# An encoder layer on one core: the first gate's weight parts without a hold, and split by GpSimd

## The chip, the cores and the metric

The kernel runs on one core of one Trainium2 chip. The core has a matrix engine (TensorE, PE in the profile), a vector engine (VectorE, DVE), an activation engine (ScalarE, ACT), a general engine (GpSimd, POOL) and a queue engine that only issues transfers (SyncE, SP). Each engine takes its own instructions strictly in order; semaphores make one wait for another. The metric is the device time of one execution in microseconds (us), lower is better.

## The reference

One bidirectional encoder layer is applied to two sequences of 1024 positions and 1024 channels, in float32. With `p = rmsnorm(x) @ w_in` cut into a Fourier value, a Fourier gate, three Hyena inputs, a Hyena gate and two merge gates, it computes

```
fz  = real(fft over positions and, per group of 256, over channels)(fv)
y_f = (fz * silu(fg)) @ w_fourier_out
v, x1, x2 = short_conv(hv)                 # width 3
z   = x2 * long_conv(x1 * long_conv(v, k0), k1)   # filters k from a small network
y_h = (z * silu(hg)) @ w_hyena_out
out = (sigmoid(mg_f) * y_f + sigmoid(mg_h) * y_h) @ w_out
y   = x + rmsnorm(out, g_post)
```

Every one of the large products has 1024 x 1024 weights per section of `w_in`, and is needed nearly exact, so each operand is kept as two parts: a rounded one (`h`) and the remainder (`l`), and a product is three matmuls, h*h, h*l and l*h.

## The kernel before

The work is traced in program order, and a planner puts it in an order per engine before the run: it keeps its own reckoning of when each operand is there, and on each engine takes the earliest-traced instruction that is ready by that reckoning. The chip then runs each engine's list in order. Four stages follow one another in the program, but the lists overlap them:

- `phase_fourier` (line 489): for both sequences, the normalized and transposed input, the Fourier values and their transforms, written to DRAM (`d_x`, `d_fz`). Its last part, called the tail here, is the second half of the second sequence: `stage` (line 423) and the channel transform (lines 458 to 487), a chain of small matmuls on TensorE, copies on ScalarE (lines 434, 475, 476) and sums on VectorE.
- The filter stage, the first loop of `phase_main` (line 928): the first sequence's input is loaded back in 8 pieces and split into `xh`, `xl` by `load_x` (line 711: cast on ScalarE, subtraction on VectorE); then 16 filters are made (`filter_taps`, `filter_spectrum`), and between them 30 gate tiles (`spill_gate`, line 793) fill TensorE. `fill` (line 925) spreads the gate tiles over the 16 rounds; round 0 has one of them, the first tile of section 5, and `self.opening` is true in that round alone.
- `branches` (line 977): the long convolutions of both sequences, with the projections between them.
- `phase_blocks` (line 1044): the second sequence's remaining projections and the output products, in an order written out by hand.

A gate tile is one call of `inproj` (line 739): two PSUM tiles (`pin`, tag `mm` with four buffers), and for each half of the weights (`q`, 512 columns) a raw tile `wr` of 256 KB fetched by SyncE into one of two buffers, a pair of rooms for its parts, and 24 matmuls that read the parts and `xh`, `xl`. The rooms rotate over four pairs (`rooms`, line 724): `wh`/`wl` twice, then two pairs called `whl` elsewhere. The parts of the first sequence's tiles are made in lines 762 to 764: ScalarE rounds the raw weights to `h`, ScalarE writes `-h` into `l`, and a transfer issued by GpSimd's queue adds the raw weights onto `l` from DRAM.

In the opening round the two ScalarE instructions stand in a block `issue_after(self.rows.ins)` (line 761), which orders them on ScalarE behind one given instruction. `self.rows` is set in line 476, each time the tail's second scaled copy `Pm` is traced; when the gate tile is traced it is the last one of the whole Fourier stage.

`split` (line 168) is the other way to make parts: a cast on ScalarE, then a subtraction raw - h on a named engine.

Of the kernel before, what the change touches and what calls it, by code (L numbers as in the profile page):

```python
# [12 lines left out]
AF = mybir.ActivationFunctionType  # L13
# [148 lines left out]
class K:  # L162
# [223 lines left out]
    def fourier_half(self, b, half, W, fo, px, pf, begun={}):  # L386

        nc = self.nc
        WE, WO = W

        def pair(shape, tag, bufs=1):
            return [pf.tile(shape, F32R, tag=f"{tag}{i}", name=f"{tag}{i}", bufs=bufs) for i in range(2)]
# [30 lines left out]
        def stage(np_, data, e, edge, out, tag):  # L423

            pe = self.psum(tag, 2, "pse")[0:np_, :258]
            po = self.psum(tag, 2, "pso")[0:np_, :258]
            for m in range(4):
                last = (edge is None and m == 1) or m == 3
                self.mm3(pe if m < 2 else po, data(m), (seq[:, 0, e, m], seq[:, 1, e, m]), m % 2 == 0, last)
                if m == 1 and edge is not None:  # L430
                    self.mm(pe.rearrange("p (a b) -> p a b", a=3), edge, al, False, True)
            ev = pf.tile([P, 258], F32, tag="sev", name="sev", bufs=1)[0:np_]
            st = pf.tile([P, 514], F32, tag="sst", name="sst", bufs=1)[0:np_]
            nc.scalar.copy(ev, pe)
            self.add("dve", st[:, 0:258], ev, po)
            if e == 0:
                self.sub("dve", st[:, 512:257:-1], ev[:, 0:255], po[:, 0:255])
            else:
                self.stt("dve", st[:, 512:257:-1], ev[:, 0:255], -1.0, po[:, 0:255])
            nc.vector.tensor_copy(st[:, 513:514], st[:, 0:1])  # L440
            if len(out) == 2:
                self.split(out[0], out[1], st, "dve", "act")
            else:
                nc.scalar.copy(out[0][0:34], st)
                self.sub("dve", out[0][32:34], st[32:34], out[0][32:34])
        ch, cx = fo["chan"], fo["chx"]
        vec = self.vec
# [6 lines left out]
        for g in range(2):  # L454
            Pp, Qp = PP[g], pair([P, 514], "qp")
            co = slice(P * g, P * g + P)
            stage(P, lambda m: (OO[0][:, m, co], OO[1][:, m, co]), 1, None, Qp, "XT"[g])
            A = pf.tile([P, 1026], F32, tag="fA", name="fA", bufs=1)
            B = pf.tile([P, 1026], F32, tag="fB", name="fB", bufs=1)
            gg = 2 * half + g  # L460
            for n in range(2):
                w = (258, 256)[n]
                ns = slice(258 * n, 258 * n + w)
                pr, qr = (Pp[0][:, ns], Pp[1][:, ns]), (Qp[0][:, ns], Qp[1][:, ns])
                pP = self.psum("X", 2, "pP")[:, :w]
                self.mm3(pP, (ch[:, 0, 0:P], ch[:, 1, 0:P]), pr, True, False)
                self.mm(pP, cx[:, 0, g, :], PX[:, ns], False, True)
                pQ = self.psum("X", 2, "pQ")[:, :w]
                self.mm3(pQ, (ch[:, 0, P:2 * P], ch[:, 1, P:2 * P]), qr, True, False)
                self.mm(pQ, ch[:, 0, 2 * P:3 * P], pr[0], False, False)  # L470
                self.mm(pQ, ch[:, 0, 2 * P:3 * P], pr[1], False, False)
                self.mm(pQ, cx[:, 1, g, :], PX[:, ns], False, True)
                Ps = pf.tile([P, 258], F32, tag="fPs", name="fPs", bufs=2)
                Pm = pf.tile([P, 258], F32, tag="fPm", name="fPm", bufs=1)
                nc.scalar.copy(Ps[:, :w], pP)
                self.rows = nc.scalar.activation(Pm[:, :w], pP, AF.Copy, scale=vec[:, 11:12])
                t0 = 258 * n
                w = (258, 255)[n]
                r = slice(0, w)
                self.stt("dve", A[:, t0:t0 + w], pQ[:, r], vec[:, 10:11], Ps[:, r])  # L480
                self.add("dve", B[:, t0:t0 + w], pQ[:, r], Pm[:, r])
                w = (258, 254)[n]
                r = slice(0, w)
                self.stt("dve", A[:, 1024 - t0:1024 - t0 - w:-1], pQ[:, r], vec[:, 11:12], Ps[:, r])
                self.stt("dve", B[:, 1024 - t0:1024 - t0 - w:-1], pQ[:, r], vec[:, 12:13], Pm[:, r])
            nc.gpsimd.dma_start(self.d_fz[b][2 * gg], A[:, 0:1024])
            nc.gpsimd.dma_start(self.d_fz[b][2 * gg + 1], B[:, 0:1024])
# [251 lines left out]
    def inproj(self, sec, mt, b=None, plain=False):  # L739

        nc, a = self.nc, self.a
        ps = [self.psum("mm", 4, f"pin{n}") for n in range(2)]
        for q in range(2):
            s = slice(512 * q, 512 * q + 512)
            src = a["w_in"][sec, mt][:, s]
            kept = self.d_w[sec - 1][mt] if b is not None else None
            if b or plain:
                h, l = [self.wp.tile([P, 512], F32R, tag=g, name=g, bufs=2) for g in ("wh", "wl")]
            else:
                h, l = self.rooms()  # L750
            if b:
                self.keep_parts()
                for t, k in zip((h, l), kept):
                    nc.sync.dma_start(t.bitcast(F32), k[:, s])
            else:
                r = self.wp.tile([P, 512], F32, tag="w", name="wr", bufs=2)
                nc.sync.dma_start(r, src)
                if plain:
                    self.split(h, l, r, "dve", "act")
                else:  # L760
                    with self.tc.issue_after(self.rows.ins) if self.opening else ExitStack():
                        nc.scalar.copy(h, r)  # L762
                        nc.scalar.mul(l, h, -1.0)
                    nc.gpsimd.dma_start(l, src, accum_op=ADD)
                    self.keep_parts()
                    if kept:
                        self.unsaved = [(t, k[:, s]) for t, k in zip((h, l), kept)]
            h, l = [t.rearrange("p (a b) -> p a b", a=4) for t in (h, l)]
            for n in range(2):
                for kk in range(4):  # L770
                    k = 4 * q + kk
                    s = slice(512 * n, 512 * n + 512)
                    self.mm3(ps[n], (h[:, kk], l[:, kk]), (self.xh[k][:, s], self.xl[k][:, s]), k == 0, k == 7)
        return ps
# [741 lines left out]
```

## Time and profile before

| | |
|---|---|
| median of three runs | 2438.34 us (2437.77 to 2440.07) |
| the profiled execution | 2444.92 us, its span 2443.1 us |
| TensorE busy | 2371.6 us, 97% of the span |
| VectorE busy | 1986.3 us, 81% |
| ScalarE busy | 1177.0 us, 48% |
| GpSimd busy | 449.3 us, 18% |
| bytes moved | 499.65 MB, mean 205 GB/s |

The span is the time from the first to the last instruction of the profiled execution; the time of that execution holds a little around it. Busy shares are means over stages, so the stretches in the prediction are read beside them. A row of the timeline has the start in us from the span's start, the duration in us, engine, line, operation, output and inputs, the shape, and in brackets the idle time of the engine before it with what ended it; rows that follow one another are merged with a count. Rows of groups have the count, total busy time and mean ns of one. Lines of helpers (171 and 181 for the split's cast and subtraction, 177, 194 for every matmul) stand for all that call them, so the tile's name tells which work it is.

### The profile page before, as it was taken

To read this page: it belongs to the slowest core of one execution; us is meant where nothing else is said; L and a number is where in the kernel's file an instruction comes from. 1 tells how busy PE (TensorE), PEld (TensorE's weight loads), DVE (VectorE), ACT (ScalarE), POOL (GpSimd) and SP (SyncE) were. 2 spreads that over 40 slices of the span, in tenths; PEclk is the share of its full clock that TensorE was granted. 3 is DMA by queue.
4 is the path that set the end of the run, shared out by engine and by line. 5 is a ranking of instruction groups with operands and counts; after the bars stand their busy time and mean duration, and the time that the engine had idled before them with its cause. 6 is when DMAs were issued, how large, how long until landed. Compare 5 with 4: busy or idle time off the path is not lost. (4 is left out here: it accounts for less than half of the span.)

```text
span 2443.1 us, 37244 instructions
## 1 busy us (share of the span) xinstructions
PE 2371.6 (97%) x13006; PEld 2058.6 (84%) x13006; DVE 1986.3 (81%) x3840; ACT 1177.0 (48%) x2220; POOL 449.3 (18%) x568
## 2 busy tenths in 40 slices
PE   5998899999999999999999999999999999999998
PEld 4987788888888888888888888888888888888786
DVE  7687777777776899899899999998667687778777
ACT  5545677776754444343332322333334375656543
POOL 1331111111122232321124444310000000101000
PEclk9998899999999999999999999999999999999999
DMA  8544876777777767665455666553646687978744
GB/s 319 171 160 173 239 198 193 202 203 198 214 213 236 203 201 203 190 180 167 172 181 181 217 208 214 190 172 135 215 147 216 213 306 248 279 263 228 224 155 155
DMA packets 262980, 499.65 MB, mean 205 GB/s; under 512 B 26550, under 2 KB 90263, under 8 KB 262408
## 3 DMA queue, kind: packets, MB, share of 16 engines
q1 hardware_dynamic: 220076, 380.53, 46.7%
q0 software_dynamic: 42528, 116.72, 18.3%
q8 instruction: 102, 1.67, 0.3%
q14 instruction: 86, 0.70, 0.1%
q10 hardware_dynamic: 188, 0.02, 0.0%
HBM read 333.59 MB, written 167.77 MB: 205 GB/s over the span
## 5 line engine op out<-in xcount | busy, mean ns | idle before, releaser
L194 PE MATMUL pin<-xh,wl 128*128 128x512 f32 x1024 | 401.7, 394 | 3.0 <-DMA wl<-in_w_in 2.4
L194 PE MATMUL pin<-xh,wh 128*128 128x512 f32 x1024 | 403.2, 394 | 0.9 <-ACT wh L762 0.9
L194 PE MATMUL pin<-xl,wh 128*128 128x512 f32 x1024 | 402.8, 393 | 0.0
L194 PE MATMUL pin<-xh,whl 128*128 128x512 f32 x896 | 292.4, 396 | 0.0
L194 PEld LDWEIGHTS pin<-xh,wl 128*128 128x128 f32 x1024 | 193.8, 189 | 38.8 <-DMA wl<-in_w_in 2.6
L194 PEld LDWEIGHTS pin<-xh,wh 128*128 128x128 f32 x1024 | 194.0, 190 | 36.1 <-ACT wh L762 1.2
L194 PEld LDWEIGHTS pin<-xl,wh 128*128 128x128 f32 x1024 | 193.9, 189 | 35.0
L194 PEld LDWEIGHTS pin<-xh,whl 128*128 128x128 f32 x896 | 167.7, 189 | 32.5
L194 PE MATMUL pT<-cinv,yh 128*128 128x256 f32 x1024 | 192.8, 283 | 2.3 <-ACT yh L171 2.3
L194 PE MATMUL pin<-xl,whl 128*128 128x512 f32 x448 | 177.7, 397 | 0.0
L194 PEld LDWEIGHTS pT<-cinv,yh 128*128 128x128 f32 x1024 | 165.5, 191 | 12.4 <-ACT yh L171 2.7
L194 PE MATMUL pX<-bh,cfwd 128*128 128x256 f32 x768 | 159.5, 288 | 1.1 <-ACT bh L171 1.1
L181 DVE TENSOR_TENSOR t<-pX,k 128x1024 f32<-128x1024 f32 x128 | 156.1, 1219 | 4.0 <-PE pX L194 3.1
L171 ACT CAST yh<-y 128x512 fp32r<-128x512 f32 x128 | 79.3, 620 | 158.1 <-DVE y L181 120.4
L194 PE MATMUL pT<-cinv,yl 128*128 128x256 f32 x512 | 145.6, 284 | 0.0
L171 ACT CAST bh<-b 128x512 fp32r<-128x512 f32 x144 | 88.9, 619 | 105.9 <-DVE b L181 69.6
L194 PEld LDWEIGHTS pX<-bh,cfwd 128*128 128x128 f32 x768 | 126.1, 192 | 4.8 <-ACT bh L171 1.6
L181 POOL TENSOR_TENSOR draw<-draw 128x256 f32<-128x256 f32 x96 | 92.4, 963 | 114.8 <-DMA draw<-in_w_out 39.8
L181 DVE TENSOR_TENSOR bl<-b,bh 128x512 fp32r<-128x512 f32 x144 | 101.3, 706 | 12.0 <-ACT bh L171 11.9
L194 PE MATMUL pX<-bl,cfwd 128*128 128x256 f32 x384 | 109.7, 286 | 0.0
L181 DVE TENSOR_TENSOR yl<-y,yh 128x512 fp32r<-128x512 f32 x128 | 90.6, 708 | 16.4 <-ACT yh L171 16.2
L194 PEld LDWEIGHTS pT<-cinv,yl 128*128 128x128 f32 x512 | 98.2, 192 | 1.9
(366 smaller groups left out, 6091.9 us busy)
## 6 DMA issues: line engine op xcount, KB each, us to landing
k<-d_k SPq DMA_DIRECT2D x128, 512.0 KB, 4.4
wr<-in_w_in SPq DMA_DIRECT2D x136, 256.0 KB, 3.5
d_g<-gt SPq DMA_DIRECT2D x92, 256.0 KB, 3.5
d_k<-kt SPq DMA_DIRECT2D x128, 128.0 KB, 2.8
d_k<-kt SPq DMA_DIRECT2D x64, 256.0 KB, 2.5
fz<-d_g SPq DMA_DIRECT2D x64, 256.0 KB, 5.5
wl<-in_w_in POOLq DMA_DIRECT2D x56, 256.0 KB, 5.2
whl<-in_w_in POOLq DMA_DIRECT2D x56, 256.0 KB, 5.4
```

What stands on the lines that cost most here:

```text
L171: self.rounded = nc.scalar.copy(h, src)
L181: return e.tensor_tensor(out, a, b, op=op)
L194: return self.nc.tensor.matmul(out, lhsT, rhs, start=start, stop=stop, skip_group_check=shared)
```

## The change

In the opening round the first gate tile's parts are now made by `split` with a subtraction on GpSimd. The hold behind the Fourier stage's last scaled copy is gone, and so are, for the two halves of this one tile, the negation on ScalarE and the accumulating transfer. All other gate tiles are made as before. The later tiles of the second sequence (`plain`) keep VectorE for the subtraction.

```diff
@@ fourier_half
-                self.rows = nc.scalar.activation(Pm[:, :w], pP, AF.Copy, scale=vec[:, 11:12])
+                nc.scalar.activation(Pm[:, :w], pP, AF.Copy, scale=vec[:, 11:12])
@@ inproj
                 r = self.wp.tile([P, 512], F32, tag="w", name="wr", bufs=2)
                 nc.sync.dma_start(r, src)
-                if plain:
-                    self.split(h, l, r, "dve", "act")
+                if plain or self.opening:
+                    self.split(h, l, r, "dve" if plain else "pool", "act")
                 else:
-                    with self.tc.issue_after(self.rows.ins) if self.opening else ExitStack():
-                        nc.scalar.copy(h, r)
-                        nc.scalar.mul(l, h, -1.0)
+                    nc.scalar.copy(h, r)
+                    nc.scalar.mul(l, h, -1.0)
                     nc.gpsimd.dma_start(l, src, accum_op=ADD)
                     self.keep_parts()
```

## The prediction

> **What bounds the kernel now.** First the page: engine totals, and the strip of 40 slices of 61 us each.
>
> ```profile
> span 2443.1 us, 37244 instructions
> ...
> PE 2371.6 (97%) x13006; PEld 2058.6 (84%) x13006; DVE 1986.3 (81%) x3840; ACT 1177.0 (48%) x2220; POOL 449.3 (18%) x568
> ...
> PE   5998899999999999999999999999999999999998
> ...
> PEclk9998899999999999999999999999999999999999
> ```
>
> TensorE is busy for 97% of the span, so work taken off it counts one for one wherever it never waits. Its clock dips in two slices only, the fourth and fifth (183 to 305 us), which is where the edited weights are used. So the next view is busy time by stretches around that place; the columns are the stretch, its length, PE, PEld, DVE, ACT and POOL busy with counts, the granted clock, the DMA share and GB/s.
>
> ```profile
> 200.00:210.00 10.00, 10.00 (x86) 10.00 (x85) 5.08 (x15) 3.24 (x8) 1.10 (x2) 1.00 0.14 55
> 210.00:220.00 10.00, 5.95 (x46) 5.21 (x45) 5.64 (x12) 5.65 (x11) 1.05 (x2) 1.00 0.85 278
> 220.00:230.00 10.00, 7.80 (x48) 6.94 (x48) 8.89 (x19) 7.32 (x12) 0.00 (x0) 0.83 1.01 388
> 230.00:240.00 10.00, 5.41 (x20) 4.32 (x20) 9.54 (x19) 6.71 (x14) 0.71 (x2) 0.54 0.55 195
> 240.00:250.00 10.00, 6.61 (x31) 5.94 (x32) 8.15 (x21) 5.88 (x15) 1.06 (x2) 0.67 0.36 125
> 250.00:260.00 10.00, 8.54 (x29) 6.56 (x28) 5.14 (x14) 8.23 (x20) 4.81 (x7) 0.59 0.68 205
> 260.00:270.00 10.00, 7.78 (x22) 6.15 (x23) 8.51 (x20) 2.36 (x7) 0.40 (x1) 0.66 1.07 318
> 270.00:280.00 10.00, 10.00 (x57) 8.69 (x56) 6.39 (x18) 7.55 (x19) 1.75 (x2) 1.00 0.84 292
> ...
> 720.00:760.00 40.00, 40.00 (x209) 34.12 (x208) 18.06 (x46) 21.02 (x39) 10.08 (x16) 1.00 0.89 268
> ...
> 1400.00:1500.00 100.00, 100.00 (x616) 89.64 (x615) 99.03 (x168) 29.76 (x56) 46.96 (x60) 1.00 0.65 216
> ```
>
> The Fourier tail is a hole in TensorE's work, and from 270 us it is full again. Between 220 and 270 us the idle time is 2.20 + 4.59 + 3.39 + 1.46 + 2.22 = 13.9 us. On top the busy time ran slow: busy times (1 - clock) gives 1.3 + 2.5 + 2.2 + 3.5 + 2.6 = 12.1 us. So about 26 us of full-rate TensorE time are lost in these 50 us. What ends the waits, in the view of waits of PE for 205 to 270 us:
>
> ```profile
> PE pQ L194 <- DVE fB L177: 5.1, 3, 2.1
> PE pft L194 <- ACT sev L434: 2.4, 1, 2.4
> PE pin L194 <- DMA wl<-in_w_in: 2.4, 1, 2.4
> ```
>
> The tail hops TensorE, ScalarE, VectorE and back with nothing to fill in between. The gate's matmuls (`pin`) would be filler, and the hold keeps them out: on ScalarE the last held-to row is L476, and the casts follow it at once.
>
> ```profile
> 250.94 0.45 ACT L476 ACTIVATE fPm<-pP,vec 128x256 f32<-128x256 f32 x1
> 251.30 1.13 ACT L762 CAST wh<-wr 128x512 fp32r<-128x512 f32 x2
> ...
> 253.13 1.14 ACT L763 ACTIVATE wl<-wh 128x512 fp32r<-128x512 f32 x2
> ```
> ```profile
> 193.74 1.21 SPq L757 DMA_DIRECT2D wr<-in_w_in  x2
> ...
> 251.93 5.67 SPq L757 DMA_DIRECT2D wr<-in_w_in  x4
> ```
> ```profile
> wr<-in_w_in SPq DMA_DIRECT2D x136, 256.0 KB, 3.5
> ```
>
> The raw weights were fetched at 193.74 us and lay for 57 us; with two raw buffers only, the next gate's weights are not fetched before 251.93 us.
>
> **The change, part by part.**
>
> *Casts no longer held.* Two casts leave 251.30 us for some point after the raw weights land, about 198 us (issued by 194.95, 3.5 us to landing at the median). ScalarE has room: 6.76 us idle in 200 to 210 alone against 1.13 us. On the path: 0; without that cover, 1.1 us. The matmuls can't follow at once, though. They read the transformed input, whose second parts VectorE makes in eight pieces, first and last:
>
> ```profile
> 221.91 1.23 DVE L181 TENSOR_TENSOR xl<-xl,xh 128x1024 fp32r<-128x1024 f32 x1
> ...
> 234.91 1.22 DVE L181 TENSOR_TENSOR xl<-xl,xh 128x1024 fp32r<-128x1024 f32 x1
> ```
>
> So the first gate can run from 223.1 us, piece by piece until 236.1 us. Its PSUM tag `mm` is free by then: the last holder of the tail is read at 209.93 us.
>
> ```profile
> 209.93 0.42 DVE L181 TENSOR_TENSOR oo<-pfv,oo 128x256 fp32r<-128x256 f32 x1 [1.44 <-ACT oo L171]
> ```
>
> What a gate costs TensorE comes from its own matmuls when they finally run:
>
> ```profile
> 262.22 0.80 PE L194 MATMUL pin<-xh,wl 128*128 128x512 f32 x1 [2.37 <-DMA wl<-in_w_in]
> ...
> 268.36 0.39 PE L194 MATMUL pin<-xh,wh 128*128 128x512 f32 x1
> ...
> 269.98 0.39 PE L194 MATMUL pin<-xl,wh 128*128 128x512 f32 x1
> ```
>
> Fourteen start between 262.22 and 268.36 us, 0.44 us each at the low clock; seven steps lead from 268.36 to 269.98 us, 0.231 us each at full. A gate is 2 halves x 2 row halves x 4 blocks x 3 products = 48 matmuls: 48 x 0.231 = 11.1 us, or 21 us cold. The room from 220 to 250 us is 10.2 us idle plus 6.0 us of slow clock, 16.2 us; so it fits if the filler also brings the clock back. Term: -11.1 us. Bounds: 0, if the matmuls end up where the tail could have run anyway; the whole 11.1 for this gate.
>
> The clock first as the rows show it: in the ten us from 220 its mean is 0.83, behind two gaps of 2.13 and 2.05 us, and it came back after 6.1 us of unbroken matmuls.
>
> ```profile
> 214.28 0.63 PE L194 MATMUL pQ<-qp,chan 128*128 128x256 f32 x3 [2.13 <-DVE fB L177]
> ...
> 220.13 0.51 PE L194 MATMUL pse<-alt,x5t 128*128 128x258 f32 x2 [2.05 <-DVE x5t L181]
> ```
>
>  The Trainium skill (TensorE: Matmul & The Clock Gate, "What's actually happening") says that the clock halves after an idle window of about 3.4 us and is restored after as long a busy one. By that rule only some 8 of the gate's matmuls would run slow rather than 14, and the sum would be better by 6 x 0.21 = 1.3 us; the rows show the slower return.
>
> *The following gate.* Two raw buffers that come free near 203 us instead of 252 us let the next gate's fetches, casts, negations and accumulating transfers start some 45 us earlier (they keep the old form). Such a transfer lands in 3.8 to 9.1 us in this stretch of the kernel:
>
> ```profile
> L764 POOL DMA_DIRECT2D wl<-in_w_in x17: 867/872/1261, 254.1 to 477.9; - x17
> ...
> DMA to landing us min/median/max: 3.8/5.1/9.1
> ```
>
> So this gate's 48 matmuls may fill what the first leaves: 16.2 - 11.1 = 5.1 us up to 250 us, and 3.7 idle + 6.1 slow = 9.8 us from 250 to 270 us. Bounds 0 and 14.9 us. I take 5, a third: the order is made by a planner in advance, and the transfer shares the DMA engines with the input's eight loads (share 0.85 and 1.01 between 210 and 230 us).
>
> *Second parts by GpSimd.* Removed: two negations on ScalarE (1.14 us for both), two issues on POOL (0.87 each) and two accumulating transfers, with TensorE's wait of 2.4 us for the first; that wait lies in the 26 us and isn't counted again. Added: two GpSimd subtractions of 128x512. None with this output is in the trace; the nearest rows, and GpSimd's first row after the fetch:
>
> ```profile
> L181 POOL TENSOR_TENSOR x<-x,sg 128x512 f32<-128x512 f32 x16 | 38.2, 2400 | 38.5 <-ACT sg L1007 38.4
> ...
> L181 POOL TENSOR_TENSOR eo<-xg 128x512 f32<-128x512 f32 x8 | 15.4, 1938 | 7.8 <-ACT xg L347 5.1 <-DVE sst L440 1.3 <-DVE el L181 1.3
> ...
> L181 POOL TENSOR_TENSOR wo<-wor,wo 128x256 fp32r<-128x256 f32 x16 | 14.4, 913 | 21.1 <-ACT wo L171 21.1
> ```
>
> ```profile
> 207.46 0.57 POOL L486 DMA_DIRECT2D d_fz<-fA  x1 [19.97 <-DVE fA L177]
> ```
>
> 1.83 us (twice the 256-wide row, the same form) to 2.40 us each; I take 1.9, so 3.8 us together. POOL has nothing for 20 us before 207.46 us, so nothing queues behind them; if they came after, the `d_fz` transfers issued at 207.46 us would wait up to 4 us, and with them the buffers fA and fB. What they can disturb is VectorE: the 260-wide sum there takes 0.42 us alone and up to 0.97 beside GpSimd.
>
> ```profile
> L181 DVE TENSOR_TENSOR wer<-wfv x6: 418/564/966, 172.8 to 188.6; 128x260 f32<-128x260 f32 x6
> ```
>
> At worst VectorE loses half of 4.8 us, 2.4 us; between 200 and 210 us alone it idles 4.9 us. Term 0, bounds 0 and +2.4. On VectorE such a subtraction takes 0.71 us, 1.2 less than on GpSimd:
>
> ```profile
> L181 DVE TENSOR_TENSOR bl<-b,bh 128x512 fp32r<-128x512 f32 x144 | 101.3, 706 | 12.0 <-ACT bh L171 11.9
> ```
>
> The Trainium skill (GPSIMD Engine Reference, "4.1 Engine selection") advises VectorE for such work, GpSimd taking about twice as long for two inputs. The trace agrees (2.7 times); by that rule 2.4 us are lost if both halves lie on the path, which with some 20 us to spare before 223 us they don't.
>
> *Whether the gain lasts.* One more stretch, from the middle of the filter stage:
>
> ```profile
> 400.00:500.00 100.00, 100.00 (x537) 86.27 (x537) 77.87 (x196) 70.51 (x154) 12.22 (x14) 1.00 0.76 209
> ```
>
> From 270 us on TensorE is full, in the filter stage as later, so work done early is time saved, unless another engine then sets the pace. VectorE works only 18.06 of 40 us between 720 and 760 us: there it waits for TensorE, with 21.9 us to give. Hence a head start up to about 22 us reaches the next stage whole.
>
> Sum: -11.1 - 5 + 0 = -16 us. Against its own execution, 2444.92 us with a span of 2443.1, that is 2429; the three timed runs lie 6.6 us lower (2438.34), so I predict 2422. A measurement here can't tell less than 0.2%, 4.9 us, from no change: faster means below 2433.5, slower above 2443.2.
>
> **Rivals.**
>
> *All of the hole is filled* (0.08): both gates warm and the third begins; the gain goes to 22 to 26 us, held by VectorE's 21.9. 2438.3 - 25 = 2413. For it: free rooms and PSUM. Against: DMA share.
>
> *Only part of the first gate* (0.18): the pieces of input come every 1.9 us, each worth 6 matmuls; TensorE stays under 60% and cold, the gate takes 21 us of a 10 us idle room. About half of 11.1 plus the saved 2.4 us wait: -8, 2430.
>
> *Given back* (0.14): the head start is lost where VectorE is the bound. For it: 99.03 of 100 us busy at 1400 to 1500 us. Against: the slack at 720 us moves VectorE's work forward too. 2438.
>
> *Slower* (0.18): TensorE takes its queue in order, and the planner places the gate's matmuls by loads as it reckons them. If it reckons the input pieces or the second gate's transfers earlier than they land, matmuls that wait for them stand ahead of the tail's. The tail's 29 us after 223 us then start as late as 236 (+13), and two transfers at 9.1 rather than 3.8 us add 10.6; less the 11.1 us of matmuls, +12.5 at most, taken as +8: 2446. It decides from waits above 11 us. For it: VectorE is 89 to 95% busy making those pieces. Against: the plan before had only one such wait, 2.4 us.
>
> **How the numbers follow.** The forecast has 0.42, with 2414 to 2430 as its own range. Faster is 0.42 + 0.08 + 0.18 = 0.68, same 0.14, slower 0.18. The range runs from 2411 (just past the filled hole) to 2443, leaving 0.05 below and 0.13 above.
>
> **What would show it.** Right: casts `wh` near 200 us on ScalarE, two GpSimd rows `wl<-wr,wh` of about 1.9 us before 207 us, `pin` matmuls from 223 us, clock back at 1.00 before 240 us, the third fetch of `wr` before 212 us, and the same order of work afterwards some 16 us sooner. Wrong: a clock still at 0.6 between 230 and 260 us (part only), long waits of PE for `xl` or `whl` (slower), or a full hole with the gaps opening behind 760 us (given back).

## The result, and the profile after

The changed kernel takes 2436.53 us (median of 22 runs, 2433.34 to 2440.61); the kernel before, run beside it, takes 2441.05 us (22 runs, 2434.41 to 2446.73). The ratio is 0.9982, with a 95% interval of 0.9975 to 0.9989: 4.4 us faster, just under the 4.9 us that the prediction took as the least difference to be told. It forecast 16 us. The profiled execution took 2440.61 us, the longest of the 22, with a span of 2438.8; that of the kernel before, 2444.92 us, lies as far above its median, so this one pair of profiles shows about the same, 4.3 us.

The page of the kernel after: span, engine totals, TensorE's strip and the strip of its clock.

```profile
span 2438.8 us, 37250 instructions
...
PE 2365.9 (97%) x13006; PEld 2055.1 (84%) x13006; DVE 1992.5 (82%) x3840; ACT 1173.9 (48%) x2216; POOL 444.1 (18%) x568
...
PE   5998999999979999999999999999999999999998
...
PEclk9999999999989999999999999999999999999999
```

The clock's dip in the fourth and fifth slices (183 to 305 us) is gone, though TensorE's own digit in the fourth is still 8. A new dip stands in the twelfth, 671 to 732 us, in TensorE's digit and in the clock. The stretches of the kernel after, in the columns used in the prediction (stretch, length, PE, PEld, DVE, ACT, POOL busy with counts, granted clock, DMA share, GB/s):

```profile
210.00:220.00 10.00, 5.01 (x42) 4.80 (x41) 3.42 (x9) 1.50 (x4) 1.20 (x3) 0.87 0.89 263
220.00:230.00 10.00, 9.46 (x58) 8.47 (x59) 6.92 (x16) 7.81 (x15) 1.05 (x2) 0.79 0.73 277
230.00:240.00 10.00, 10.00 (x56) 8.59 (x55) 9.65 (x17) 8.79 (x13) 0.72 (x2) 1.00 0.80 300
240.00:250.00 10.00, 10.00 (x54) 8.61 (x54) 5.07 (x11) 4.61 (x10) 1.79 (x2) 1.00 0.76 229
250.00:260.00 10.00, 10.00 (x53) 8.53 (x52) 4.50 (x12) 8.36 (x18) 1.98 (x3) 1.00 0.84 233
260.00:270.00 10.00, 10.00 (x56) 8.72 (x55) 4.78 (x12) 6.31 (x14) 1.52 (x2) 1.00 0.62 186
...
640.00:680.00 40.00, 34.55 (x189) 29.66 (x188) 33.71 (x94) 26.42 (x65) 6.11 (x8) 0.94 0.62 170
680.00:720.00 40.00, 30.95 (x152) 26.77 (x152) 33.21 (x79) 21.45 (x46) 2.88 (x4) 0.77 0.38 115
720.00:760.00 40.00, 40.00 (x215) 34.31 (x215) 26.97 (x72) 22.28 (x45) 10.68 (x16) 1.00 0.97 287
```

And one stretch of the kernel before, which the prediction did not look at:

```profile
640.00:720.00 80.00, 80.00 (x421) 68.61 (x420) 64.49 (x160) 49.05 (x105) 16.84 (x23) 1.00 0.75 207
```

The prediction's own measure, idle time plus busy time times (1 - clock), is called lost time from here on. From 210 to 270 us it falls from 30.1 us to 8.2: in each of the four stretches from 230 us on the change leaves TensorE full at full clock. That is 21.9 us won. Between 640 and 720 us, where the kernel before loses nothing, the kernel after idles 5.45 + 9.05 = 14.5 us and runs 34.55 x 0.06 + 30.95 x 0.23 = 9.2 us' worth of slow clock: 23.7 us lost. Between them the two places leave the kernel after 1.8 us behind; that it is faster all the same comes from stretches that neither the edit nor the prediction was about (the table).

Lost time by stage, summed in this way over stretches of 10 to 100 us of each kernel's profile, is the table on which the experiments rest. The span less all lost time is 2350 to 2356 us in every one of the fourteen kernels, so the lost time accounts for the span to about 6 us. Its size depends a little on the stretches, since the clock is a mean over each: cut into stretches of 10 us, the 23.7 us become 21.3.

| lost us in | 0–210 | 210–270 | 270–600 | 600–800 | 800–1600 | 1600–end | span |
|---|---|---|---|---|---|---|---|
| before | 33.7 | 30.1 | 0 | 0 | 10.1 | 16.2 | 2443.1 |
| after | 36.1 | 8.2 | 0 | 23.7 | 4.2 | 15.7 | 2438.8 |

The rows add up to 90.1 and 87.9 us, so the table holds 2.2 of the 4.3 us; the largest term in favour of the kernel after, behind the hole, is 800 to 1600 us, which no experiment explains.

What happens at 640 to 720 us. Most of TensorE's idle time there, by the view of its waits for that stretch of the kernel after (what waits, for what; us, times, the longest):

```profile
PE pft L194 <- DVE T L181: 9.8, 4, 5.8
PE pXf L194 <- ACT w3s L171: 2.4, 1, 2.4
PE pXf L194 <- DVE bl L181: 1.5, 1, 1.5
```

`pft` and `pXf` are the filter network's small matmuls; they wait for VectorE's and ScalarE's steps of the same chain. There is no filler left between them: from 668.01 to 697.81 us every matmul of TensorE is the filter network's. The end of the filler shows in the timelines of the kernel after: the last gate tile ahead of the two projections is copied out at 638.18 us, the last matmul of the two projections is issued at 667.78 us, and the projections' four PSUM tiles are read only from 689.82 us, behind a sum of the filter's own work.

```profile
638.18 0.59 ACT L801 COPY gt<-pin 128x512 f32<-128x512 f32 x1 [2.13 <-PE pin L194]
...
689.82 1.27 ACT L783 ACTIVATE v<-pin,wsh 128x512 f32<-128x512 f32 x2 [1.79 <-DVE fO L181]
```
```profile
667.78 0.39 PE L194 MATMUL pin<-xh,whl 128*128 128x512 f32 x1
```

The kernel before copied that same gate tile 38 us later:

```profile
676.33 0.59 ACT L802 COPY gt<-pin 128x512 f32<-128x512 f32 x1 [2.13 <-PE pin L194]
```

The filters went the other way. Each filter's taps end in a sum `fE` on VectorE, behind which its spectrum is made; the first and the last of the 16, before and then after:

```profile
259.20 1.21 DVE L181 TENSOR_TENSOR fE<-T,T 128x1024 f32<-128x1024 f32 x1
...
702.91 1.22 DVE L181 TENSOR_TENSOR fE<-T,T 128x1024 f32<-128x1024 f32 x1
```
```profile
280.50 1.22 DVE L181 TENSOR_TENSOR fE<-T,T 128x1024 f32<-128x1024 f32 x1
...
716.67 1.23 DVE L181 TENSOR_TENSOR fE<-T,T 128x1024 f32<-128x1024 f32 x1
```

So the gates finish 38 us sooner and the filters 14 us later. The time from the last gate's copy ahead of the projections to the last filter's sum, called the gap from here on, grows from 702.9 - 676.3 = 26.6 us to 716.7 - 638.2 = 78.5 us. The theory to be tested (the gap theory): for the length of the gap TensorE has only two projections and the filters' small matmuls to do; past some length it starves and its clock falls. Rivals: the PSUM tiles that the two projections hold block gates that could run; the GpSimd subtraction rather than the missing hold delays the filter chain; or VectorE's load in later stages takes the gain back, as the prediction's own rival had it.

### The profile page after: what moved, and what is told of

It reads as the page before. It is cut to its first block, busy times and chain, and to the rows that moved or that the text cites. A ratio compares the mean times of both kernels' runs of the same rounds, so it can differ in the third digit from the quotient of the medians.

```text
span 2438.8 us, 37250 instructions
## 1 busy us (share of the span) xinstructions
PE 2365.9 (97%) x13006; PEld 2055.1 (84%) x13006; DVE 1992.5 (82%) x3840; ACT 1173.9 (48%) x2216; POOL 444.1 (18%) x568
## 5 line engine op out<-in xcount | busy, mean ns | idle before, releaser
L181 POOL TENSOR_TENSOR draw<-draw 128x256 f32<-128x256 f32 x96 | 98.1, 1022 | 112.8 <-DMA draw<-in_w_out 38.7
L181 DVE TENSOR_TENSOR bl<-b,bh 128x512 fp32r<-128x512 f32 x144 | 104.2, 726 | 14.6 <-ACT bh L171 14.5
```

The lines of the kernel that those rows point to most:

```text
L181: return e.tensor_tensor(out, a, b, op=op)
```

## The experiments

All kernels compute the complete result; only order and the making of parts differ. Ratios are to the kernel before, run on the same chip.

**Which of the two edits.** `unhold_only` drops the hold and leaves the parts to negation and accumulating transfer; `hold_pool` keeps the hold on the cast and makes the second part on GpSimd.

```diff
unhold_only, against before:
-                    with self.tc.issue_after(self.rows.ins) if self.opening else ExitStack():
-                        nc.scalar.copy(h, r)
-                        nc.scalar.mul(l, h, -1.0)
+                    nc.scalar.copy(h, r)
+                    nc.scalar.mul(l, h, -1.0)
hold_pool, against after (line 476 sets self.rows again, as before):
-                    self.split(h, l, r, "dve" if plain else "pool", "act")
+                    with ExitStack() if plain else self.tc.issue_after(self.rows.ins):
+                        nc.scalar.copy(h, r)
+                    self.sub("dve" if plain else "pool", l, r, h)
```

> The hold is taken away, the parts are still made by negation and accumulating transfer; the result is complete. If the hold alone matters, the hole between 228 and 270 us is filled as in the changed kernel (TensorE busy 10 of 10 us from 230 us, clock 1.00) and the ratio to the kernel before is within 0.2% of the changed kernel's 0.998. If GpSimd's subtraction is what lets the gate start early, the first gate's matmuls wait for transfers that land 4 to 9 us after their issue and the ratio is 1.000 or above.

> The hold on the rounding cast stays, the second parts are made by GpSimd's subtraction. Only the wait of 2.4 us for the first accumulating transfer near 262 us can go; the hole stays. Ratio to the kernel before 0.999 to 1.000 if the hold is what matters; 0.998 if the subtraction is.

Measured: `unhold_only` 2436.57 us against 2443.3, ratio 0.9971 (0.9961 to 0.9982); `hold_pool` 2442.96 us, 1.0004 (0.9995 to 1.0014). In the profile of `unhold_only` 8.5 us are lost from 210 to 270 us and 23.4 us from 600 to 800, with a gap of 714.7 - 636.8 = 78 us: the whole picture of the change. `hold_pool` has 24.7 and 0, with a gap of 26.6 us; the 5.4 us that its hole loses less than before are lost again behind it (5 to 6 us from 270 to 600 us). So the hold alone does it, the gain and the giving back, and GpSimd's subtraction brings nothing that can be told. The rival that blamed the subtraction falls.

**PSUM or the gap.** `after_gates_first` traces the last round's two gate tiles one round sooner, ahead of the two projections, so that they need no tile that the projections hold. `before_gates_first` does it to the kernel before.

```diff
+            cut = lambda i: i * len(fill) // nf if i < nf - 1 else len(fill)
...
-                for sec, c in fill[i * len(fill) // nf:(i + 1) * len(fill) // nf]:
+                for sec, c in fill[cut(i):cut(i + 1)]:
```

> The changed kernel, with the last round's two gate tiles traced in the round before, ahead of the first two convolution projections. Theory 1 (the gain is lost because those two projections sit in all four PSUM tiles until filter 14 gives back its tap tiles, and TensorE has no filler from 668 to 712 us): the 14.5 us of idle time and about 9 us of slow clock between 640 and 720 us go, 22 us of gate matmuls fill them, ratio 0.990 to 0.994. Theory 2 (the filters start 21 us later and the last of them, at 717 us, sets when the next stage begins, whatever fills the time before): ratio 0.997 to 0.999, the last filter again at about 717 us.

> The kernel before, with the same two gate tiles moved ahead of the projections. There TensorE is full from 270 to 800 us, so there is no idle time to win back: both theories expect 0.998 to 1.002. A gain like that of the changed kernel with this edit would say that the edit is worth its gain by itself and not as the return of a lost head start.

Measured: `after_gates_first` 2437.3 us, 0.9982 (0.9973 to 0.9991), and `before_gates_first` 2442.28 us, 0.9999 (0.999 to 1.0007). Neither is told apart from the kernel that it was made of. In `after_gates_first` the last gate is copied at 668.2 us instead of 638.2, but the loss only falls from 23.7 to 16.2 us, for the last filter ends still later; neither expectation had that. Stretches and last sum of `after_gates_first`:

```profile
640.00:680.00 40.00, 37.33 (x201) 32.01 (x199) 28.04 (x77) 28.75 (x57) 8.41 (x12) 1.00 0.81 233
680.00:720.00 40.00, 33.79 (x151) 27.48 (x151) 32.60 (x79) 26.84 (x62) 8.66 (x13) 0.83 0.60 170
```
```profile
731.97 1.22 DVE L181 TENSOR_TENSOR fE<-T,T 128x1024 f32<-128x1024 f32 x1
```

Here no gate is left for a held tile to block, and still 16.2 us are lost: the tiles can't be the main cause. They do have a part. In the kernel after the next gate's first matmul is issued at 697.81 us, when the last reading of a held tile by VectorE ends (697.01 + 0.74 us); but at most the 7.5 us that the edit saves can be put down to them. The two gates' work, some 22 us by the prediction's 11.1 each, bought 7.5 us in the stage, since it pushed the last filter 15.3 us later, from 716.67 to 731.97 us.

**Gates traced a round later.** If the filters lose because the gates stand in their way, giving the filters the earlier place in the trace should help. `after_gates_later1` and `after_gates_later2` shift all gates by one and two rounds, `before_gates_later1` does it to the kernel before.

```diff
+            cut = lambda i: max(i - 1, 0) * len(fill) // nf if i < nf else len(fill)
...
-                self.opening = i == 0
-                for sec, c in fill[i * len(fill) // nf:(i + 1) * len(fill) // nf]:
+                for sec, c in fill[cut(i):cut(i + 1)]:
+                    self.opening = (sec, c) == fill[0]
```

> The changed kernel, with every gate tile traced one filter round later, so that the planner prefers the next filter to a gate. Theory 2 (the gates took the lead of the filters; the filters, which start 21 us later and keep 29.5 us a round, end the stage, with TensorE short of work from 640 to 720 us): the filters run ahead again, the last one is at 700 us or earlier, no idle time between 640 and 720 us, ratio to the kernel before 0.990 to 0.995. Theory 1 (only the PSUM tiles held by the first two projections keep the late gates out): those projections are still ahead of four gates, so TensorE still idles there, ratio 0.997 to 1.000.

> The same by two rounds: a second dose. Theory 2: filters still earlier, ratio 0.988 to 0.995; if the gates then run out of time behind the last filter, six of them stand at the end with nothing of the filters to cover and the ratio rises to that of one round or above. Theory 1: 0.997 to 1.002.

> The kernel before with the gates one round later: the control. It keeps the hole at 210 to 270 us, and its TensorE is full in the filter stage, so theory 2 expects 0.998 to 1.002. A gain here as large as with the change would mean that the order of gates and filters is worth it by itself.

Measured: 1.0063 (1.0047 to 1.0079), 1.0132 (1.0115 to 1.0148) and 1.0049 (1.0036 to 1.0062): slower, all three. This missed. The first filter's sum of `after_gates_later1` is at 279.0 us, hardly sooner than 280.5, so the place in the trace is not what put the gate ahead of it. And the shift leaves only 26 gates ahead of the projections where there were 28, so the last of them is copied at 607.1 us and the gap grows to 101 us, with 37.9 us lost from 600 to 800 (55.9 in `after_gates_later2`). `before_gates_later1` holds the useful point: its last filter ends at 703.6 us, as in the kernel before, only the last gate comes sooner (648.0), the gap is 56 us, and 7.9 us are lost where the kernel before loses none.

**The gap from the other side.** `before_filter_late` leaves the gates of the kernel before alone and delays the filters, by holding the copy of the filter network's hidden layer behind the Fourier tail.

```diff
-            nc.scalar.copy(self.hid, hid)
+            with tc.issue_after(self.rows.ins):
+                nc.scalar.copy(self.hid, hid)
```

> The kernel before with one thing delayed: ScalarE's rounding of the hidden layer, which every filter matmul reads, is held behind the tail as the gate is (251 us in place of 215). The first filter's matmuls then start at about 253 us in place of 233 and its sums come at 275 to 282 us in place of 259, without any filler brought forward. If the late first filter is what the stage pays for at its end, TensorE runs short between 640 and 720 us as in the changed kernel, and the ratio is 1.004 to 1.008. If the filters catch up on the way, the ratio is 0.999 to 1.002.

Measured: 2445.49 us, 1.0015 (1.0005 to 1.0025). First and last sum of `before_filter_late`, and its stretch:

```profile
286.22 1.23 DVE L181 TENSOR_TENSOR fE<-T,T 128x1024 f32<-128x1024 f32 x1
...
729.01 1.23 DVE L181 TENSOR_TENSOR fE<-T,T 128x1024 f32<-128x1024 f32 x1
```
```profile
680.00:720.00 40.00, 36.74 (x185) 31.32 (x184) 31.93 (x79) 23.56 (x56) 4.10 (x5) 0.87 0.56 137
```

The last gate is at 673.0 us, so the gap is 56 us, made almost wholly by late filters, and 3.26 us idle plus 36.74 x 0.13 of slow clock is 8.0 us lost: the same gap and the same loss as `before_gates_later1` reached by early gates. The filters did not catch up (27.0 us late at the first sum, 26.1 at the last), yet the ratio lies in the range expected for filters that do: in the profile, 4.0 us lost at 270 to 600 and the 8.0 here stand against 9.4 us less between 800 and 1600 us (0.7 against 10.1).

**Filler back into the gap.** `after_more_gates` adds two of the branch stage's gate tiles to the 30, ahead of the projections.

```diff
+            fill[28:28] = [(4, 6), (4, 7)]
+            cut = lambda i: i * 30 // nf + 2 * (i >= nf - 1)
...
-                early = c < NH
+                early = True
```

> The changed kernel with two more gate tiles in the filter stage, traced in the last round but one: the two of section 4 (channels 6 and 7 of eight) that are otherwise computed in the branch stage, where TensorE is full. They are filler from outside the stage, 96 matmuls or 22 us. If the head start is lost for want of filler between the last gate (638 us) and the last filter (717 us), they fill most of the 23.7 us lost there without any tile missing afterwards, and the branch stage is up to 22 us shorter: ratio 0.990 to 0.995. If filler put there only pushes the last filters back, as the two tiles moved inside the stage did (717 to 732 us), the last filter is at 730 us or later and the ratio is 0.997 to 1.000.

Measured: 2445.08 us against 2441.11, 1.0016 (1.0005 to 1.0026), outside both expected ranges. Stretches of `after_more_gates`:

```profile
680.00:720.00 40.00, 36.91 (x184) 30.92 (x183) 31.91 (x78) 25.14 (x54) 4.31 (x6) 0.91 0.54 144
...
760.00:800.00 40.00, 34.55 (x215) 30.88 (x214) 26.14 (x45) 13.79 (x24) 11.15 (x15) 0.97 0.77 234
...
1300.00:1400.00 100.00, 94.21 (x563) 82.72 (x562) 96.38 (x169) 29.47 (x56) 40.74 (x51) 0.98 0.59 188
```

In its own place it does what the gap theory says: last gate 667.6 us, gap 57 us, 640 to 720 us loses 6.4 instead of 23.7. But 6.5 us are lost from 760 to 800 us, and 23.6 from 800 to 1600 us where the kernel after loses 4.2. The likely reading is that the two tiles were filler where they came from: filler is a fixed amount here, and moved, it leaves a hole. That is not shown apart from two other things: the profiled execution, 2453.0 us, is the slowest of eleven and 7.9 us above their median, and the two tiles now also go out to DRAM and back.

**How much of the hold to give up.** Three kernels free the first gate tile and hold later ones behind the same copy: `after_hold_next` the second round's two, `after_hold_third` only the second of these, `unhold_hold_next` as the first of them, but with all parts by negation and accumulating transfer.

```diff
unhold_hold_next, against before:
-                self.opening = i == 0
+                self.opening = i == 1
after_hold_next, against after (line 476 sets self.rows again; after_hold_third: self.second for fill[2] only):
-                    nc.scalar.copy(h, r)
-                    nc.scalar.mul(l, h, -1.0)
+                    with self.tc.issue_after(self.rows.ins) if self.second else ExitStack():
+                        nc.scalar.copy(h, r)
+                        nc.scalar.mul(l, h, -1.0)
...
-                self.opening = i == 0
+                self.opening, self.second = i == 0, i == 1
```

> The changed kernel, with the hold put on the two gate tiles of the next round instead: only the first gate's 48 matmuls (11.1 us) can enter the tail. If the filler of the following gates is what delays the tail and the first filter (its sums at 280 us in place of 259), that filter comes at 262 to 270 us, TensorE idles less than 10 us between 640 and 720 us, and the ratio is 0.994 to 0.997. If the first gate alone delays it, the filter stays at 275 to 280 us and the ratio is 0.998 to 1.000.

> The changed kernel with the hold on the third gate tile alone: gates one and two are free to fill the tail. A dose between the change (first filter at 280 us, ratio 0.998) and the hold on gates two and three (260 us, 0.996). If each gate let into the tail pushes the first filter back, it comes between 264 and 276 us and TensorE idles for 3 to 12 us between 640 and 720 us, ratio 0.995 to 0.998. If only the third gate did the harm, the first filter is at 260 to 263 us and the ratio is 0.992 to 0.995, since 22 us of work then lie in the hole.

> The kernel before with the hold moved from the first gate tile to the two of the next round; all parts by negation and accumulating transfer. If GpSimd's subtraction adds nothing to the gain, the first gate fills the hole as with the changed kernel and its hold on the next gates, and the ratio is within 0.15% of that kernel's 0.996. If the subtraction is needed to have the first gate in time, the ratio is 0.998 to 1.000.

Measured: `after_hold_next` 2429.8 us against 2442.81, 0.9958 (0.9944 to 0.9972); `unhold_hold_next` 2430.63 us against 2441.8, 0.9952 (0.9939 to 0.9965); `after_hold_third` 2436.48 us, 0.9977 (0.9969 to 0.9986). The first two aren't told apart, and both beat the kernel before and the changed one; the interval of `after_hold_third` still overlaps that of `after_hold_next` a little. Stretches of `after_hold_next`, with its first and last sum:

```profile
220.00:270.00 50.00, 39.18 (x188) 32.38 (x189) 39.80 (x86) 31.37 (x65) 6.98 (x11) 0.83 0.78 259
...
640.00:720.00 80.00, 80.00 (x426) 68.77 (x425) 62.40 (x151) 49.65 (x108) 15.55 (x22) 1.00 0.76 210
...
800.00:1600.00 800.00, 799.48 (x4799) 710.79 (x4797) 761.71 (x1353) 288.05 (x501) 259.82 (x307) 1.00 0.63 195
```
```profile
259.86 1.22 DVE L181 TENSOR_TENSOR fE<-T,T 128x1024 f32<-128x1024 f32 x1
...
712.12 1.23 DVE L181 TENSOR_TENSOR fE<-T,T 128x1024 f32<-128x1024 f32 x1
```

With only the first gate in the hole, 20.3 us are lost from 210 to 270 us, 9.8 fewer than before; the first filter's sum stays at 259.86 us; the last gate is at 670.1 us, the gap is 42 us, and 640 to 720 us is full. All kernels in the order of the gap, with one profile each; the profiled execution lies between 0.8 us below and 7.9 us above the median of its kernel (2429.03 against 2429.8 us for `after_hold_next`, 2440.34 against 2436.48 for `after_hold_third`), so differences of spans overstate some differences of medians:

| kernel | last gate, us | last filter, us | gap, us | lost 600–800 | lost 210–270 | lost 800–1600 | span |
|---|---|---|---|---|---|---|---|
| before_gates_first | 703.1 | 701.0 | -2 | 0 | 27.3 | 10.8 | 2443.8 |
| before | 676.3 | 702.9 | 26.6 | 0 | 30.1 | 10.1 | 2443.1 |
| hold_pool | 677.8 | 704.4 | 26.6 | 0 | 24.7 | 5.9 | 2442.3 |
| unhold_hold_next | 668.0 | 709.1 | 41 | 0 | 20.2 | 1.6 | 2428.8 |
| after_hold_next | 670.1 | 712.1 | 42 | 0 | 20.3 | 0.5 | 2427.2 |
| after_hold_third | 665.7 | 721.0 | 55 | 7.1 | 15.4 | 1.1 | 2438.6 |
| before_gates_later1 | 648.0 | 703.6 | 56 | 7.9 | 29.8 | 8.5 | 2453.2 |
| before_filter_late | 673.0 | 729.0 | 56 | 8.0 | 30.2 | 0.7 | 2445.6 |
| after_more_gates | 667.6 | 724.5 | 57 | 12.9 (6.4 to 720 us) | 8.7 | 23.6 | 2451.2 |
| after_gates_first | 668.2 | 732.0 | 64 | 16.2 | 8.5 | 6.4 | 2438.2 |
| unhold_only | 636.8 | 714.7 | 78 | 23.4 | 8.5 | 2.7 | 2434.6 |
| after | 638.2 | 716.7 | 78.5 | 23.7 | 8.2 | 4.2 | 2438.8 |
| after_gates_later1 | 607.1 | 707.9 | 101 | 37.9 | 8.5 | 6.5 | 2453.6 |
| after_gates_later2 | 577.5 | 705.3 | 128 | 55.9 | 8.2 | 6.8 | 2471.2 |

The loss from 600 to 800 us follows the gap whichever side moves it: nothing up to 42 us, 6 to 8 us at 55 to 57 (in `after_more_gates` counted to 720 us, ahead of the hole that its moved filler left), 16 at 64, 24 at 78, 38 at 101, 56 at 128. From 56 us on it grows by about 0.67 us for each us of gap. An estimate from the rows agrees: before, a filter takes 29.6 us, in which TensorE, full, does 30/16 gates of 11.1 us, so the filters' own matmuls are about 0.3 of its time and the other 0.7 of any further gap is lost.

`after_hold_third`, with one filler gate more than `after_hold_next`, wins 4.9 us more in the hole (15.4 against 20.3), and loses 7.1 in the gap and 6.8 more from 270 to 600 us (10.0 against 3.2): in these two profiles the second gate's filling is worth less than it costs.

## Why the prediction was wrong

**What bounded the kernel** was read rightly: the hole from 220 to 270 us, the hold as what kept the filler out, the clock as half of the loss. The lost time that it worked out there, 26 us, is 30.1 with the ten us from 210.

**Casts, fetch and clock** came as forecast. Timelines of the kernel after, ScalarE, SyncE and GpSimd:

```profile
201.24 0.61 ACT L171 CAST wh<-wr 128x512 fp32r<-128x512 f32 x1
202.40 0.62 ACT L171 CAST wh<-wr 128x512 fp32r<-128x512 f32 x1
```
```profile
196.61 11.74 SPq L757 DMA_DIRECT2D wr<-in_w_in  x6
```
```profile
201.93 2.55 POOL L181 TENSOR_TENSOR wl<-wr,wh 128x512 fp32r<-128x512 f32 x2 [11.58 <-ACT wh L171]
```

The casts are at 201 and 202 us (near 200 was forecast), the fetches into freed buffers are issued by 208.35 us (before 212), and the clock is 1.00 from 230 us (before 240). The first gate's matmuls begin at 228.59 us rather than 223, since the tail and the input behind it came some 6 us later (below); they still fit.

**Second parts by GpSimd**: the price of nothing was right, and `hold_pool` shows it by itself. The two subtractions took 1.29 us each where 1.9 was taken, and were done by 204.48 us, 24 us before their first reader.

**The first gate's term**, -11.1 us, was about right. `after_hold_next` leaves just this gate in the hole, and its hole loses 9.8 us less.

**"The following gate" failed.** The step gave it -5 us with bounds of 0 and -14.9. It filled more than that: the hole gave 21.9 us in all, 12 beyond the first gate alone, so in the hole itself the forecast was too low and "all of the hole is filled" was nearest. What the bounds left out is a price. The filler is not only worth what it fills: it goes through in-order queues ahead of the tail and of the first filter. The trace shows it at three engines, before and then after:

```profile
213.01 0.43 DVE L181 TENSOR_TENSOR fB<-pQ,fPm 128x258 f32<-128x258 f32 x1 [1.05 <-DMA d_fz<-fB]
214.69 1.04 ACT L913 CAST hid<-hidr 128x1024 fp32r<-128x1024 f32 x1
233.26 0.79 PE L194 MATMUL pft<-w3s,hid 128*128 128x256 f32 x2 [2.44 <-ACT sev L434]
```
```profile
205.79 0.62 ACT L761 CAST whl<-wr 128x512 fp32r<-128x512 f32 x1 [2.51 <-DMA wr<-in_w_in]
207.52 0.92 POOL L763 DMA_DIRECT2D whl<-in_w_in  x1 [3.04 <-ACT oo L171]
210.34 0.57 POOL L486 DMA_DIRECT2D d_fz<-fA  x1 [0.25 <-DVE fA L177]
216.36 0.48 DVE L177 SCALAR_TENSOR_TENSOR fA<-pQ,vec,fPs 128x258 f32<-128x258 f32 x1 [3.14 <-DMA d_fz<-fA]
218.85 0.43 DVE L181 TENSOR_TENSOR fB<-pQ,fPm 128x258 f32<-128x258 f32 x1 [2.00 <-DMA d_fz<-fB]
220.53 1.04 ACT L912 CAST hid<-hidr 128x1024 fp32r<-128x1024 f32 x1
244.93 0.40 PE L194 MATMUL pft<-w3s,hid 128*128 128x256 f32 x2
```

ScalarE stands idle for 2.51 us until the raw weights for the following gate's cast land, with the tail's copies queued behind that cast. Two of that gate's transfers go out ahead of the tail's `d_fz` (207.46 us before, 210.34 after), and VectorE then waits 3.14 and 2.00 us for the buffers that `d_fz` frees, where it waited 1.05. So the copy of the filter network's hidden layer `hid` is 5.8 us late. The prediction had weighed such a delay of `d_fz`, but for GpSimd's subtractions alone, and put it at nothing. By the first filter's matmul, with the gates' matmuls ahead of it on TensorE, it is 11.7 us. The tail's last transfer is issued at 271.09 us where it was 252.57, and the first filter's sum comes at 280.50 instead of 259.20. The filter chain is a second long chain beside TensorE's, 16 filters, one sum every (702.91 - 259.20) / 15 = 29.6 us before and every 29.1 after, and nothing in it catches up fast: 21.3 us late at the first, 13.8 at the last. Holding just these gates gives that time back: 0.9958 instead of 0.9982, with intervals that just keep apart. The same two gates, let loose, won 12 us in the hole and lost 24 at 640 to 720.

**"Whether the gain lasts" failed too.** VectorE's 21.9 idle us at 720 to 760 us were read as VectorE waiting for TensorE, hence as room for a head start. But the last filter's sum is at 702.91 us: by 720 us only the end of that filter's spectrum is left (4.5 us of the waits), and most of the idle time belongs to the projection and the convolution behind it. From VectorE's waits in those 40 us of the kernel before:

```profile
DVE bs L181 <- ACT xt L822: 7.3, 2, 3.7
DVE v L177 <- ACT v L784: 7.0, 1, 7.0
```

The stretch to look at was the last one in which the filters run, 640 to 720 us. There VectorE works 64.49 of 80 us and TensorE is full only because gates are left. A head start for the gates alone shortens their part and leaves the filters where they are, or later. The head start passes only while the gap can be filled.

**The rivals.** "Given back" was right in kind, and its time, 2438, is closest to the result. Its place was wrong: it put the loss at 1400 to 1500 us where VectorE is 99% busy, but the branch stage loses less after (4.2 against 10.1 us), and the loss is at 640 to 720 us, where TensorE waits for steps of the filter chain (9.8 us for VectorE's `T` alone) though VectorE is busy for only 33.71 and 33.21 of 40 us. "Slower", by matmuls that wait at the head of TensorE's queue, did not happen: the longest wait from 205 to 275 us is 5.1 us, for the tail's own `fB`, which was late for want of its buffer as shown above.

```profile
PE pQ L194 <- DVE fB L177: 5.1, 1, 5.1
```

**Where luck comes in.** That the time fell at all was forecast, but not for the reason that the profiles give: gain in the hole and loss in the gap leave -1.8 us, and the direction rests on the later stages, which stay open.

**What stays open.** The lost time between 800 and 1600 us varies from 0.5 to 10.8 us between kernels whose program there is the same, and it makes up 9.6 of the 16 us by which the span of `after_hold_next` is ahead of that of the kernel before (the medians differ by 13.0 us). It is read off, not explained: no run held the earlier stages fixed and changed this one. In the kernel after, 2.4 us more are lost ahead of 210 us than before (36.1 against 33.7); the variants of it have 34 to 37 there with the same program up to that point, so one profile of each doesn't say whether this belongs to the change. Why the first filter comes at 279 to 281 us wherever these gates are free, even when they are traced a round later, is settled only in part: `after_hold_next` shows that holding them keeps it at 259.86, and the rows above account for the first 11.7 of the 21.3 us; the rest was not followed.

## What to carry to other kernels

Where filler is a fixed amount, as it was here, a hole filled with work pulled ahead is no gain by itself: the filler is missed later, and where it is missed must be looked up before the gain is booked. Take the two chains that have to meet (here the gates on TensorE and the filters across three engines), read from the profile when each ends, and ask what runs between these two ends once one is earlier; lost time by stage, idle plus busy times (1 - clock), shows the transfer at once where busy shares don't. When a hold is lifted, try holding the next thing in line: here it kept the filler in the hole to one piece and left the second chain its start.

## What the runs showed of the hardware

GpSimd's subtraction of 128x512 with the rounded output type took 1.29 us, in another place of the program (`hold_pool`) 1.30. Rows of the kernel after and of `hold_pool`, by group:

```profile
L181 POOL TENSOR_TENSOR wl<-wr,wh 128x512 fp32r<-128x512 f32 x2 | 2.5, 1292 | 11.6 <-ACT wh L171 11.6
```
```profile
L181 POOL TENSOR_TENSOR wl<-wr,wh 128x512 fp32r<-128x512 f32 x2 | 2.6, 1298 | 7.6 <-ACT wh L760 7.6
```

That is well under the 1.83 to 2.40 us that the prediction took from its nearest rows, and 1.8 times VectorE's 0.706 us for the same shape. The Trainium skill (GPSIMD Engine Reference, "4.1 Engine selection") puts two inputs at about twice VectorE's time; these rows agree better with it than the prediction's 2.7 times, which was no measurement but its own estimate of 1.9 us over 0.71.

The clock's price came on top of the gaps': of the 23.7 us lost at 640 to 720 us, 14.5 are gaps of up to 5.8 us, and 9.2 are matmuls at the lower clock behind them.
